# RWKV chain: the output sums move to a PSUM bank alone, the state sums move to the bank of the other sums

## The chip, the cores and the metric

The kernel runs as one program on one core of a Trainium2 chip. The metric is the device time of one execution in microseconds (us). Three runs of the kernel before took 1316.70, 1319.14 and 1324.66 us, so the median is 1319.14 us. The execution that the profile shows took 1316.68 us, of which 1314.9 us are the span from the first instruction of the program to the last.

## What is computed

One layer of a streaming encoder, for a prompt of 1024 positions and for 64 new positions with a past of 512. A projection gives the columns of three branches: an RWKV-7 recurrence (A), attention with forget gates (B) and sparse attention over selected keys (C, whose selection is a top-k search). The branches are gated, concatenated and multiplied by an output matrix. The change lies in the recurrence of branch A, which the reference states step by step:

```
def step(S, inp):
    r_t, w_t, k_t, v_t, kk_t, a_t = inp
    sa = einsum('bhij,bhj->bhi', S, -kk_t)
    S = S * w_t + sa (kk_t * a_t) + v_t k_t          # outer products
    return S, einsum('bhij,bhj->bhi', S, r_t)
wkv, y = lax.scan(step, wkv0, ...)
```

There are 8 heads of 64 by 64 state. The kernel takes 64 positions (a chunk) at a time, so that a step of its chain is four products for one pair of heads, and the next chunk needs the state that this one leaves.

## The kernel before, in words

The program lists instructions in an order of its own. A scheduler then puts the instructions of each engine in a fixed order of issue; it puts a ready instruction ahead of one whose inputs it expects later, and it sets semaphore waits between engines. It treats two accesses by different engines to one tile in PSUM as dependent when they lie in the same bank, even where they touch different columns, so a matmul into a bank waits until a read of that bank that stands ahead of it is done. On the chip each engine issues strictly in that order.

The time from about 160 to 760 us is a weave of several parts, started by `program` through `braid`. There are 17 units of four chunks (16 of the prompt, one of the new positions), and in each round of the loop run: `chain` of one unit, `chunk_invert` and `value_rows` of the next, `prepare` of the one after (`elem`, `chunk_rows`), and `tail` of the one before. Beside them `topk` searches the 256 best keys of branch C on DVE and ACT, and then writes one mask for each block of queries (lines L656 to L669, seven masks, of widths from 1024 down to 384, and 576 for the new positions). Between all of these, `pump` lays down pieces of the big projection (L154, three matmuls for each piece) on PE. `tied` keeps such a piece, and a piece of the search, from being issued ahead of the part that it was laid behind.

One step of `chain` does this, for a pair of heads, `h` being 0 and 1:

- **pa** (L1572): the old state times a chunk's rows, into bank gd; DVE adds a term to give `za` (L1573), while ACT scales the old state to `sp` (L1574).
- **pb** (L1577): `za` times the inverted matrix, into bank gd; DVE copies it in two halves to `UV` (L1582).
- **ps** (L1585): the sum that updates the state, into bank gc; DVE makes the new state `S` from it and `sp` (L1590).
- **py** (L1594) and **pyS** (L1596): two parts of the chunk's output, the second from the old state, into another part of bank gc. After four steps ACT copies all four outputs out at once to `Yt` (L1600).

The matmuls pa, pb and pyS have 64 by 64 weights, so each takes one quarter of PE's array; ps and py have 128 by 64, one half of it. All of them are float32, which the trace shows as two passes for each matmul, so a pair for both heads appears as x4.

Names that the rows and the order use: `ps_gc` and `ps_gd` are the tiles of the banks gc and gd; `BA`, `QR`, `UD`, `P` are operands of the chain; `ps_gb` with `U`, `T`, `Y`, `ND` (L1484, L1491, L1498, L1522, L1527, L1531) is `chunk_invert`; `ps_ga` (L107, L1376, L1425, L1434, L1470) is `prepare` and `value_rows`; `pproj` (L154) is the projection; `eq`, `cum`, `sg`, `nm` are the search's masks. PEld is the loading of weights into PE's array.

Of the kernel before, what the change touches and what calls it, by code (L numbers as in the profile page):

```python
# [18 lines left out]
OP = mybir.AluOpType  # L19
# [66 lines left out]
class K:  # L86
# [1461 lines left out]
    def chain(self, one, slots, x):  # L1548

        nc, I, O = self.nc, self.I, self.O  # L1550
        v, g, sc = nc.vector, nc.gpsimd, nc.scalar
        G = self.gring("gc", 1)
        hv = (slice(0, 64), slice(64, 128))
        i64 = self.con[:, C_I64:C_I64 + 64]
        QR, UD, P1, BA, UV, Pt = x["QR"], x["UD"], x["P1"], x["BA"], x["UV"], x["Pt"]
        sample = slots[0][1] == 16
        s0 = x.get("s0")
        if sample:
            send = one.tile([P, 256], F32, tag="e1", name="s_end").rearrange("p (c t) -> p c t", t=64)
        Yt = one.tile([P, 4, 64], F32, tag="Yt", name="Yt", bufs=2)  # L1560
        ends = []
        ch, ab = G(), self.gring("gd", 1)()
        for c, (hp, t) in enumerate(slots):
            S = s0[:, hp] if sample else self.state
            if t == 0:
                S = one.tile([P, 64], F32, tag="S", name="S", bufs=2)
                v.memset(S, 0.0)

            za, sp = [one.tile([P, 64], F32, tag=n, name=n) for n in ("za", "sp")]
            pa, pb = [ab[:, 256 * i + c * 64:256 * i + c * 64 + 64] for i in range(2)]  # L1570
            for h in range(2):
                nc.tensor.matmul(pa[hv[h]], QR[hv[h], c, 1], S[hv[h]], start=True, stop=True)  # L1572
            v.tensor_tensor(za, pa, P1[:, c], op=OP.add)  # L1573
            sc.activation(sp, S, AF.Copy, scale=Pt[:, c, 64:65])  # L1574
            yield
            for h in range(2):
                nc.tensor.matmul(pb[hv[h]], UD[hv[h], c], za[hv[h]], start=True, stop=True)  # L1577
            for h in range(2):
                if UA >> h & 1:
                    sc.copy(UV[hv[h], h, c], pb[hv[h]])  # L1580
                else:
                    v.tensor_copy(UV[hv[h], h, c], pb[hv[h]])  # L1582
            yield
            for h in range(2):
                nc.tensor.matmul(ch[hv[h], c * 64:c * 64 + 64], BA[:, h, c, 64 * h:64 * h + 64], UV[:, h, c], start=True, stop=True)  # L1585
            if sample:
                self.state = send[:, c]
            else:
                self.state = one.tile([P, 64], F32, tag="S", name="S", bufs=2)
            v.scalar_tensor_tensor(self.state, ch[:, c * 64:c * 64 + 64], Pt[:, c, 64:65], sp, op0=OP.mult, op1=OP.add)  # L1590

            py = ch[:, 256 + c * 64:320 + c * 64]
            for h in range(2):
                nc.tensor.matmul(py[hv[1 - h]], BA[:, h, c, 64 - 64 * h:128 - 64 * h], UV[:, h, c], start=True, stop=False)  # L1594
            for h in range(2):
                nc.tensor.matmul(py[hv[1 - h]], QR[hv[h], c, 0], S[hv[h]], start=False, stop=True)  # L1596
            if t >= 15:
                ends.append((hp, self.state))
            yield
        sc.copy(Yt, ch[:, 256:512].rearrange("p (c t) -> p c t", t=64))  # L1600
        if ends:
            ps = self.tp()
            n = len(ends)
            so = one.tile([64, n, P], F32, tag="QR" if sample else "so", name="so", bufs=3 if sample else 1)
            for i, (hp, s2) in enumerate(ends):
                nc.tensor.transpose(ps[0:64, i * P:i * P + P], s2, self.ident)
            sc.copy(so, ps[0:64, :n * P].rearrange("p (c t) -> p c t", t=P))
            dst = O["s_a_wkv" if sample else "p_a_wkv"][0, 0, 2 * slots[0][0]:2 * slots[0][0] + 2 * n]
            nc.sync.dma_start(out=dst.rearrange("(c h) v d -> v c h d", h=2), in_=so.rearrange("v c (h d) -> v c h d", h=2))
            yield  # L1610
        x.update(Yt=Yt)
# [318 lines left out]
```

## Time and profile before

| what | value |
|---|---|
| runs, median (lowest to highest) | 1319.14 us (1316.70 to 1324.66) |
| profiled execution | 1316.68 us |
| its span | 1314.9 us, so 1.8 us lie around it |
| PE (matmuls) busy | 1261.2 us, 96% of the span |
| DVE busy | 846.3 us, 64% |
| ACT busy | 781.1 us, 59% |
| POOL busy | 672.1 us, 51% |
| mean granted clock of PE | 0.984 |

The weave lasts from about 160 to 760 us. After it come the attention of branches B and C and the output products, up to the end. PE's busy time counts a matmul from its start to its modelled end, so overlapping matmuls count once. The granted clock is a share of full speed: 1.00 is 2.4 GHz, and half of it 1.2 GHz.

### The profile page before, as it was taken

What the parts mean: (1) busy time and instruction counts of PE and PEld (TensorE: products, weight loads), DVE (VectorE), ACT (ScalarE), POOL (GpSimd) and SP (SyncE); (2) the same over time, 40 slices, a digit from 0 to 9 for tenths busy, and PEclk for the clock granted to TensorE, in tenths of its full rate; (3) what the DMA queues carried; (4) which work ended last, traced back from release to release, by engine and by line L of the source; (5) the groups of instructions that cost most, each with busy time, mean ns of one, the idle gap of its engine ahead of it and who ended that gap; (6) DMA issues with size and microseconds to landing.
All of it is one profiled execution on the core that took longest, in us unless ns stands there. A gap on an engine that the chain in (4) does not pass through costs nothing.

```text
span 1314.9 us, 29369 instructions
## 1 busy us (share of the span) xinstructions
PE 1261.2 (96%) x10563; PEld 965.1 (73%) x10563; DVE 846.3 (64%) x2487; ACT 781.1 (59%) x1762; POOL 672.1 (51%) x973
## 2 busy tenths in 40 slices
PE   7999999999999999989999998999999988999997
PEld 5777777767777767767777677888888766777764
DVE  7378357887777678888654226555665588666642
ACT  7355357867777878534343356676665577655532
POOL 6333444544554556545463474567667477544311
PEclk9999999999999999988999998999999989999999
DMA  7432421232142325324243479777646475533323
GB/s 226 114 94 70 131 83 51 72 90 70 57 127 71 97 88 161 97 88 133 68 142 102 137 202 264 204 205 224 183 146 184 134 212 173 151 107 109 94 77 96
DMA packets 171700, 168.79 MB, mean 128 GB/s; under 512 B 38641, under 2 KB 146209, under 8 KB 171426
## 3 DMA queue, kind: packets, MB, share of 16 engines
q1 hardware_dynamic: 171554, 166.91, 43.7%
q8 instruction: 84, 1.38, 0.4%
q14 instruction: 62, 0.51, 0.1%
HBM read 106.18 MB, written 62.25 MB: 128 GB/s over the span
## 4 chain that ended last, share of the span: by engine, by line
PE 56%; DVE 7%; DMA 3%; ACT 3%; issue 1%; POOL 1%; SPq 0%; DVEq 0%; POOLq 0%; ACTq 0%
PE pproj L154 21%; PE pproj L1710 7%; PE ps_pv L995 5%; PE ps_atp L107 4%; PE ps_tp L1710 4%; PE ps_sc L964 2%; PE ps_sc L965 2%; PE ps_ga L1425 2%; PE ps_tp L107 1%; PE ps_gb L1484 1%; PE ps_gb L1491 1%; PE ps_gc L1594 1%; PE ps_gc L1585 1%; ACT junka L603 1%; PE ps_gc L1596 1%
## 5 line engine op out<-in xcount | busy, mean ns | idle before, releaser
L154 PE MATMUL pproj<-uH,wh 128*128 128x384 f32 (+4 forms) x1088 | 494.4, 454 | 0.0
L154 PE MATMUL pproj<-uH,wl 128*128 128x384 f32 (+4 forms) x1088 | 363.7, 334 | 0.0
L154 PE MATMUL pproj<-uL,wb 128*128 128x384 bf16 (+4 forms) x1088 | 358.9, 330 | 0.9 <-DVE shift L808 0.5
L154 PEld LDWEIGHTS pproj<-uH,wh 128*128 128x128 f32 (+1 forms) x1088 | 217.3, 200 | 4.1 <-issue 0.4
L154 PEld LDWEIGHTS pproj<-uH,wl 128*128 128x128 f32 (+1 forms) x1088 | 207.7, 191 | 2.4 <-issue 0.2
L154 PEld LDWEIGHTS <-wb 128*128 128x128 bf16 (+1 forms) x1088 | 106.3, 98 | 117.0 <-issue 80.4
L603 ACT ACTIVATE junka<-score,tk_tau 128x1024 f16<-128x1024 f32 (+4 forms) x160 | 149.3, 933 | 42.3 <-DVE tk_tau L617 26.4
L916 POOL TENSOR_SCALAR S<-S,mx 128x128 f32<-128x128 f32 (+8 forms) x136 | 105.0, 775 | 82.8 <-DVE mx L915 58.8
L140 POOL TENSOR_TENSOR wl<-wraw,wh 128x256 fp32r<-128x256 f32 (+1 forms) x184 | 137.6, 779 | 6.9 <-ACT wh L137 4.9
L933 ACT CAST hl<-ps_atp 128x512 fp32r<-128x512 f32 (+3 forms) x184 | 93.6, 515 | 80.0 <-PE ps_atp L107 71.0
L934 DVE TENSOR_TENSOR hl<-ps_atp,hl 128x512 fp32r<-128x512 f32 (+3 forms) x184 | 109.7, 600 | 45.6 <-ACT hl L933 43.9
L911 ACT ACTIVATE S<-S,mx 128x128 f32<-128x128 f32 (+8 forms) x136 | 105.8, 778 | 39.5 <-DVE mx L907 36.1
L995 PE MATMUL ps_pv<-hl,VS 128*128 128x256 f32 (+3 forms) x640 | 113.8, 290 | 7.2 <-ACT hl L933 3.1
L142 POOL TENSOR_SCALAR wb<-wraw 128x512 bf16<-128x512 f32 (+1 forms) x92 | 61.4, 685 | 106.7 <-issue 63.9
L995 PEld LDWEIGHTS ps_pv<-hl,VS 128*128 128x128 f32 (+1 forms) x640 | 90.6, 176 | 20.1 <-DVE hl L934 4.6
L107 PE MATMUL ps_atp<-ident,S 128*128 128x128 f32 x616 | 103.4, 279 | 1.1 <-POOL S L916 0.8
L1161 POOL TENSOR_TENSOR cb<-nm,T 128x256 f32<-128x256 bf16 (+2 forms) x80 | 56.3, 710 | 55.8 <-DVE mx L907 54.2
L107 PEld LDWEIGHTS ps_atp<-ident,S 128*128 128x128 f32 x616 | 76.3, 143 | 7.8 <-issue 1.7
L1710 PE MATMUL pproj<-oh,gh 128*128 128x512 f32 x144 | 67.4, 490 | 1.1 <-ACT oh L1689 0.8
L137 ACT CAST wh<-wraw 128x1024 fp32r<-128x1024 f32 (+1 forms) x46 | 47.7, 1037 | 33.0 <-PE pproj L154 32.4
L1710 PE MATMUL pproj<-ol,gb 128*128 128x512 bf16 (+1 forms) x144 | 52.4, 386 | 0.9 <-DVE ol L1690 0.9
L1710 PE MATMUL pproj<-oh,gl 128*128 128x512 f32 x120 | 46.7, 399 | 0.0
(383 smaller groups left out, 2834.1 us busy)
## 6 DMA issues: line engine op xcount, KB each, us to landing
wraw<-in_w_in_dram SPq DMA_DIRECT2D x45, 512.0 KB
oraw<-in_w_out_dram SPq DMA_DIRECT2D x12, 512.0 KB
out_dram<-rows SPq DMA_DIRECT2D x10, 512.0 KB
x<-in_x_prompt_dram SPq DMA_DIRECT2D x8, 512.0 KB
wt<-a_wa SPq DMA_DIRECT2D x16, 256.0 KB
b_v<-vs SPq DMA_DIRECT2D x8, 512.0 KB
VS<-b_v SPq DMA_DIRECT2D x8, 512.0 KB
d_y<-y SPq DMA_DIRECT2D x64, 64.0 KB
```

What stands on the lines that cost most here:

```text
L107: self.nc.tensor.transpose(out, x, self.ident[:n, :n])
L140: nc.gpsimd.tensor_tensor(l[:, k:k + 2, :n], raw[:, k:k + 2, :n], h[:, k:k + 2, :n], op=OP.subtract)
L142: nc.gpsimd.tensor_scalar(b[:, k:k + 4, :n], raw[:, k:k + 4, :n], 1.0, 0.0, op0=OP.mult, op1=OP.add)
L154: self.nc.tensor.matmul(ps[:n, :nt], a[:, k, :n], b[:, k, t0:t0 + nt], start=(k == 0 and i == 0), stop=(k == KD - 1 and i == 2))
L603: nc.scalar.activation(junk[:, :sc.shape[1]], sc, AF.Sign, bias=tf[:, j:j + 1], accum_out=cnt[:, j:j + 1])
L911: nc.scalar.activation(S[:, :kn], S[:, :kn], AF.Exp, bias=mx[:, nm - 1:nm], scale=-1.0, accum_out=mx[:, 6:7])
L916: nc.gpsimd.tensor_scalar(S[:, :kn], S[:, :kn], mx[:, 7:8], 0.5, op0=OP.mult, op1=OP.mult)
L933: nc.scalar.copy(ph[:kr, a:b], ps[:kr, a:b])
L934: nc.vector.tensor_tensor(pl[:kr, a:b], ps[:kr, a:b], ph[:kr, a:b], op=OP.subtract)
L995: nc.tensor.matmul(pv[0:m, q0:256], VS[:, kb, 0:m], hl[:, x, o:o + w], start=kb == 0 and x == 0, stop=at[-1][0] == last and n == 3)
L1161: nc.gpsimd.tensor_tensor(o, x, y, op=OP.add)
L1710: nc.tensor.matmul(ps[hf][:n, :], parts[m // 4][q][:, m % 4, :n], self.wo[m][q // 2][:, hf * 512:hf * 512 + 512], start=m == 0 and q == 0, ...
```

## The change

The chain had two PSUM tiles: `ch` in bank gc held the four state sums and the four outputs, and `ab` in bank gd the four pa and the four pb. Now `py4` in bank gc holds the four outputs alone. `ab` holds two pa and two pb, used in turn by even and odd steps, and the four state sums behind them. The arithmetic, the operands and the number of instructions on every engine are the same: each engine has the same instructions before and after, in another order.

```diff
-        ch, ab = G(), self.gring("gd", 1)()
+        py4, ab = G(), self.gring("gd", 1)()
...
-            pa, pb = [ab[:, 256 * i + c * 64:256 * i + c * 64 + 64] for i in range(2)]
+            pa, pb = [ab[:, 128 * i + c % 2 * 64:128 * i + c % 2 * 64 + 64] for i in range(2)]
+            ps = ab[:, 256 + c * 64:320 + c * 64]
...
-                nc.tensor.matmul(ch[hv[h], c * 64:c * 64 + 64], BA[:, h, c, 64 * h:64 * h + 64], UV[:, h, c], start=True, stop=True)
+                nc.tensor.matmul(ps[hv[h]], BA[:, h, c, 64 * h:64 * h + 64], UV[:, h, c], start=True, stop=True)
...
-            v.scalar_tensor_tensor(self.state, ch[:, c * 64:c * 64 + 64], Pt[:, c, 64:65], sp, op0=OP.mult, op1=OP.add)
-
-            py = ch[:, 256 + c * 64:320 + c * 64]
+            v.scalar_tensor_tensor(self.state, ps, Pt[:, c, 64:65], sp, op0=OP.mult, op1=OP.add)
+
+            py = py4[:, c * 64:c * 64 + 64]
...
-        sc.copy(Yt, ch[:, 256:512].rearrange("p (c t) -> p c t", t=64))
+        sc.copy(Yt, py4[:, :256].rearrange("p (c t) -> p c t", t=64))
```

Behind the changed place the lines are numbered two higher: pa is L1574 after, pb L1579, ps L1587, `S` L1592, py L1596, pyS L1598.

The first place is PE, the chain's 38th step, from ps to the next step's pa. Before:

```order
L1585 MATMUL ps_gc<-UV,BA 64x64 x2
L1491 LDWEIGHTS ND_1698
L1491 MATMUL ps_gb<-T_7810,ND_1698 128x64
...
L1425 MATMUL ps_ga<-QR,BK 128x128 x4
L1594 MATMUL ps_gc<-UV,BA 64x64 x2
L1596 MATMUL ps_gc<-S,QR 64x64 x2
L1572 MATMUL ps_gd<-S,QR 64x64 x2
```

With the change:

```order
L1596 MATMUL ps_gc<-UV,BA 64x64
L1587 MATMUL ps_gd<-UV,BA 64x64 x2
L1596 MATMUL ps_gc<-UV,BA 64x64
L1598 MATMUL ps_gc<-S,QR 64x64 x2
L1425 MATMUL ps_ga<-QR,BK 128x128 x4
L1491 LDWEIGHTS ND_1698
L1491 MATMUL ps_gb<-T_7810,ND_1698 128x64
...
L1574 MATMUL ps_gd<-S,QR 64x64 x2
```

The py and pyS matmuls moved up to the ps matmuls, and the same eight other matmuls that stood between ps and py now stand between pyS and the next pa.

The second place is DVE, where the search writes its first mask (width 1024). Before:

```order
L656 TENSOR_SCALAR eq,tk_need<-sg 128x1024
L1522 TENSOR_TENSOR Y_8843<-ps_gb,con 128x256
L1380 SCALAR_TENSOR_TENSOR QR<-zt,par,ps_ga 128x4x64
L1590 SCALAR_TENSOR_TENSOR S<-ps_gc,Pt,sp 128x64
L657 TENSOR_TENSOR tk_need<-tk_need,tk_cnt 128x1
L664 SCALAR_TENSOR_TENSOR cum<-one_383,eq 128x1024
L1384 TENSOR_TENSOR BK<-kp,Pi 128x4x64
L1391 SCALAR_TENSOR_TENSOR rk<-zt,par,kp 128x256
L1382 TENSOR_TENSOR BK<-QR,tha 128x4x64
```

With the change:

```order
L656 TENSOR_SCALAR eq,tk_need<-sg 128x1024
L1349 TENSOR_SCALAR ass<-ps_ga 128x4
L1522 TENSOR_TENSOR Y_8615<-ps_gb,con 128x256
L657 TENSOR_TENSOR tk_need<-tk_need,tk_cnt 128x1
L664 SCALAR_TENSOR_TENSOR cum<-one_383,eq 128x1024
L1359 SCALAR_TENSOR_TENSOR L<-con,lw 128x260
L658 TENSOR_SCALAR tk_need<-tk_need 128x1
L1584 COPY UV<-ps_gd 64x64 x2
L667 SCALAR_TENSOR_TENSOR sg<-cum,tk_need,sg 128x1024
L1531 TENSOR_TENSOR U_8649<-U_8581,ps_gb 128x256
L1592 SCALAR_TENSOR_TENSOR S<-ps_gd,Pt,sp 128x64
L669 TENSOR_SCALAR nm<-sg 128x1024
```

The mask stands earlier against the chain: the search's last mask (L669, 64x576) is behind the 50th new state of the chain before, and behind the 48th with the change; from the first L656 to that last mask DVE makes six new states before and five with the change.

## Rows read from the trace of the kernel before

**Rows 1.** The page: engines' busy time, and PE's granted clock in 40 slices.

```profile
PE 1261.2 (96%) x10563; PEld 965.1 (73%) x10563; DVE 846.3 (64%) x2487; ACT 781.1 (59%) x1762; POOL 672.1 (51%) x973
...
PEclk9999999999999999988999998999999989999999
```

**Rows 2.** Stretches: length, busy us of PE, PEld, DVE, ACT, POOL; granted clock, DMA.

```profile
160.00:560.00 400.00, 388.69 (x4459) 292.43 (x4459) 300.75 (x966) 297.43 (x679) 203.38 (x317) 1.00 0.29 88
560.00:620.00 60.00, 51.60 (x501) 38.54 (x497) 51.24 (x119) 23.40 (x57) 33.35 (x46) 0.83 0.38 114
```

**Rows 3.** PE's waits, 200 to 780 us: total us, times, longest us.

```profile
PE ps_ga L1434 <- DVE BA L1429: 4.8, 2, 2.5
...
PE ps_gc L1594 <- DVE S L1590: 0.9, 3, 0.4
...
PE ps_gc L1594 <- DVE s_end L1590: 0.6, 2, 0.5
```

**Rows 4.** Timeline of PEld: start us, us, operation, count; py, pyS and pa.

```profile
216.37 0.20 PEld L1594 LDWEIGHTS ps_gc<-UV,BA 128*64 128x64 f32 x4 [0.31 <-DVE S L1590]
216.63 0.14 PEld L1596 LDWEIGHTS ps_gc<-S,QR 64*64 64x64 f32 x2
216.65 0.14 PEld L1572 LDWEIGHTS ps_gd<-S,QR 64*64 64x64 f32 x2
...
216.91 0.10 PEld L154 LDWEIGHTS <-wb 128*128 128x128 bf16 x1
```

**Rows 5.** Timeline of PEld: one pyS and one pa that stand apart.

```profile
450.61 0.20 PEld L1596 LDWEIGHTS ps_gc<-S,QR 64*64 64x64 f32 x4
450.87 0.11 PEld L1606 LDWEIGHTS ps_tp<-ident,S 128*64 128x64 f32 x1
...
161.80 0.20 PEld L1572 LDWEIGHTS ps_gd<-S,QR 64*64 64x64 f32 x4 [0.17 <-issue]
162.07 0.19 PEld L154 LDWEIGHTS pproj<-uH,wl 128*128 128x128 f32 x1
```

**Rows 6.** Timeline of PEld: L1376 alone, then ps directly ahead of it.

```profile
299.38 0.41 PEld L1376 LDWEIGHTS ps_ga<-ident,arn 128*64 128x64 f32 x8 [0.18 <-issue]
299.96 0.19 PEld L154 LDWEIGHTS pproj<-uH,wl 128*128 128x128 f32 x1 [0.17 <-issue]
...
236.84 0.20 PEld L1585 LDWEIGHTS ps_gc<-UV,BA 128*64 128x64 f32 x4 [0.25 <-DVE shift L808]
236.96 0.42 PEld L1376 LDWEIGHTS ps_ga<-ident,arn 128*64 128x64 f32 x8
237.55 0.20 PEld L1484 LDWEIGHTS <-U 64*64 64x64 f16 x8 [0.17 <-issue]
```

**Rows 7.** Timeline of PEld: L1484 alone, then pb directly ahead of it.

```profile
190.87 0.20 PEld L1484 LDWEIGHTS <-U 64*64 64x64 f16 x8 [0.25 <-issue]
...
191.24 0.20 PEld L107 LDWEIGHTS ps_ga<-ident,BK 128*128 128x128 f32 x2
...
241.85 0.19 PEld L1577 LDWEIGHTS ps_gd<-za,UD 64*64 64x64 f32 x4 [0.20 <-issue]
...
242.36 0.10 PEld L154 LDWEIGHTS <-wb 128*128 128x128 bf16 x1
```

**Rows 8.** Timeline of all engines, inside the stretch of the masks.

```profile
567.82 0.41 DVE L1522 TENSOR_TENSOR Y<-ps_gb,con 128x256 f16<-128x256 f32 x1
...
568.28 0.31 PE L1484 MATMUL ps_gb<-Y,U 64*64 64x64 f16 x8 [1.58 <-DVE Y L1522]
```

**Rows 9.** Instructions by line: ns least/median/most, first and last start us.

```profile
L656 DVE TENSOR_SCALAR_CACHE_REDUCE eq<-sg x7: 543/819/1205, 556.9 to 614.4; 128x1024 f16<-128x1024 f16 x1, 128x896 f16<-128x896 f16 x1, 128x768 f16<-128x768 f16 x1, 128x640 f16<-128x640 f16 x1
...
L669 DVE TENSOR_SCALAR nm<-sg x7: 260/360/597, 568.6 to 624.7; 128x1024 bf16<-128x1024 f16 x1, 128x896 bf16<-128x896 f16 x1, 128x768 bf16<-128x768 f16 x1, 128x640 bf16<-128x640 f16 x1
...
L1585 PE MATMUL ps_gc<-UV,BA x272: 219/222/369, 207.7 to 744.5; 128*64 128x64 f32 x136
```

## The prediction

> **What bounds the kernel.** I read the busy shares first. PE is busy for 1261.2 of 1314.9 us [rows 1], so the time is PE's own work, plus 54 us in which it stands, plus what it loses at a lower clock. Then the stretches of the weave, since the change lies there. From 160 to 560 us PE is busy for 388.69 of 400 us at a granted clock of 1.00: 2.8% of idle time, while DVE is at 75% [rows 2]. From 560 to 620 us it is another picture: PE is busy for 51.60 of 60 us at a clock of 0.83, and DVE has gone up to 85%. So there are two regimes. In the first, only what occupies PE counts. In the second, PE waits for DVE: at 568.28 us a matmul of `chunk_invert` starts 1.58 us late because DVE's `Y` came only at 567.82 us [rows 8]. The seven masks of the search lie there, from 556.9 to 624.7 us [rows 9]. Then the waits: the one that the change removes, py for the read of the state sum in the same bank, costs PE 0.9 and 0.6 us in the whole weave [rows 3]. It is small, because the order of issue puts other matmuls between ps and py. Last, the timeline of weight loads, which shows what a group of small matmuls costs PE.
>
> **The change part by part.** Each engine has the same instructions as before, so no work goes away. What changes is their order, and with it which matmuls stand beside each other on PE. That has a price here: when the next matmul uses another cut of the array (128x128, 128x64, 64x64), its weights are loaded only after the group before has run through. I measure a group from its first load to the first load of the next.
>
> *The 128x64 groups.* Before, ps and py stood apart; py alone takes 216.37 to 216.63, 0.26 us [rows 4], and ps has the same shape. With the change py and ps stand together. What the second pair costs then is seen where ps stands ahead of L1376, which has the same cut: the two take 0.71 us (236.84 to 237.55), L1376 alone 0.58 us (299.38 to 299.96) [rows 6], so the pair adds 0.13 us in place of 0.26. Counted along PE's whole order, groups of this cut fall from 368 to 304. 64 x 0.13 = **8.3 us less**.
>
> *pyS and pa.* Before, pyS and the next pa stood side by side. They use four different quarters of the array, and the rows show them loaded within 0.02 us of each other: all of it takes 216.63 to 216.91, 0.28 us [rows 4]. Apart, pyS takes 0.26 us and pa 0.27 us [rows 5], so parting them costs 0.25 us. In the order they share a group in 59 of 68 steps before, and in 5 with the change: 54 x 0.25 = **13.5 us more**.
>
> *What comes back.* The groups of 64x64 rise only by 23 (251 to 274), not by 54, since 31 of the freed ones stand beside other matmuls of that cut. pb ahead of L1484 shows what it saves: together 0.51 us (241.85 to 242.36), L1484 alone 0.37 us (190.87 to 191.24) [rows 7], so pb adds 0.14 in place of 0.26 or 0.27 us. 31 x 0.12 = **3.7 us less**. The groups of 64x128 rise by 3 (48 to 51); a split group costs at most another small group's 0.26 us, so 0 to 0.8, of which I take **0.4 us more**. The number of 128x128 groups, 488, stays.
>
> The rows' sum is 13.5 - 8.3 - 3.7 + 0.4 = **+1.9 us**. The Trainium skill, "TensorEngine Tiling (Array Packing)", Key Properties, says that a change of tiling mode drains the engine and that different tiles work in parallel. By the first half alone one would count groups: 1165 before and 1127 with the change, which would make it a gain of some 38 x 0.13 = 4.9 us. The second half speaks against the change, and the trace bears it out with 0.28 against 0.53 us, so I keep +1.9.
>
> *The wait.* py's wait goes, 1.5 us in all [rows 3]. But the next pa needs `S` itself, and now stands as the first matmul that does. It has the same eight other matmuls ahead of it that py had in the place shown. So the wait moves: a gain of 1.5 us if pa is never late, and as much lost again if it is late twice as often. I take **-0.5**. The Trainium skill, "Perfetto Trace Analysis", Optimizing Tensor Performance, advises rotating independent groups through banks so that a read overlaps the next matmuls; by that rule alone the whole 1.5 us would be saved, 1.0 us below my sum. Behind PE's waiting pa stands the projection; it is not needed soon. Three other new neighbours in bank gd cost nothing: ps comes after the copies to `UV` that it needs anyway, pa after the `S` that it needs anyway, and a slot that comes round after two steps was read long ago. The copy to `Yt` (ACT) no longer has the state sums in its bank.
>
> *The masks.* The search now runs up to two or three steps ahead of the chain, and its masks meet other parts of the units: the first no longer stands among the products of `elem` (L1380 to L1391). The sum of DVE's work is the same, so I take **0**. The bounds are the two rivals below: -16.9 and +17.6 us.
>
> Behind the weave PE's order is the same but for some 110 of 3,600 instructions of attention and output that change places; I take 0 for them. SP's order shifts with them, and no DMA is added.
>
> Sum against the profiled execution: 1316.68 + 1.9 - 0.5 = **1318.1 us**. That execution was at the low end of the runs; the median is 1319.14, 2.5 us higher. I give **1318**.
>
> **The rivals.**
>
> *A, faster: the stretch of the masks clears.* From 560 to 620 us PE stood for 8.4 us, and a clock of 0.83 means that 34% of it, 20.4 us, ran at 1.2 GHz instead of 2.4, which loses 10.2 us of work: 18.6 us in all [rows 2]. At the rate of the stretch before it would lose 2.8% of 60, or 1.7 us. If the masks fall on lighter parts of the units, and `S` no longer holds py back, up to 16.9 us go: 1301.2. For it: the first mask's new neighbours on DVE are few. Against it: DVE's work is not less, and the second mask takes over those products.
>
> *B, slower: the masks press closer.* From the first L656 to the last L669 DVE now makes five new states instead of six, so about one step's work of PE is no longer there to stand beside the same masks. A step takes (744.5 - 207.7) / 67 = 8.0 us [rows 9]. Where DVE is the bound, PE stands for that much more in this stretch, and there each us of standing came with 10.2 / 8.4 = 1.2 us lost to the clock: 8.0 x 2.2 = 17.6 us, 1335.7. It decides once DVE's 85% in the stretch leaves no gap of its own, so that each mask delays `chunk_invert`. Against it: PE's projections are laid at the same pace, and DVE still had 9 us free in 60.
>
> *C: the groups do not save what I count.* If py and ps in the mixed order (py, ps, ps, py) still cost 0.26 us each, and the 31 neighbours save nothing because one of the two waits, 8.3 + 3.7 us are not given back: 1330.1, likelier half of it, about 1324.
>
> That the change does nothing is excluded: the order shows py ahead of `S`.
>
> **How the numbers follow.** Forecast 0.67, with its own range of 1309 to 1327 (half of what the masks can do either way). A 0.14, B 0.11, C 0.08. A change under 1% (13 us) is about what a measurement of this kernel cannot tell from none. A gives the chance of faster, 0.14. B and a little of C, 0.03, lie above 1%: slower 0.14. The forecast and the rest of C are within it: 0.72. The range of 1304 to 1331 holds the forecast and C, a third of A and a sixth of B, and leaves out 0.18.
>
> **What would show it.** Right: in the profile after, a group of py and ps takes about 0.39 us and a lone pyS about 0.26; py waits for nothing on DVE, and pa has a wait of 1 to 2 us in total in its place; from 160 to 560 us PE stays at 97% busy and the chain's last ps comes within 8 us of 744.5. Wrong: PE's idle time or its clock between 540 and 640 us differ by over 8 us from the 8.4 and 10.2 here (A or B), a group of py and ps of 0.5 us (C), or new stretches of a lower clock in the attention, where I counted nothing.

## The result, and the profile after

The changed kernel takes 1326.57 us in the median of 19 runs (1320.76 to 1331.05), the kernel before 1317.56 us in 19 runs beside it (1312.04 to 1325.86). The ratio is 1.0061, with a 95% interval of 1.0047 to 1.0076: the change costs about 8 us (6 to 10). That is within 1%, and inside the range, but it is a slowdown where I forecast none.

The profiled execution took 1322.52 us. Its page answers to [rows 1]:

```profile
PE 1259.3 (95%) x10563; PEld 963.6 (73%) x10563; DVE 843.8 (64%) x2487; ACT 779.8 (59%) x1762; POOL 666.0 (50%) x973
...
PEclk9999999999999999999999998999999989999999
```

The instructions are the same in number, and PE is busy for 1.9 us less than before, while the span grew by 5.8 us. So PE stands more. The windows say where; the third is new here. The columns are the length, then busy time with instructions of PE, PEld, DVE, ACT and POOL, the granted clock, the DMA share and GB/s. The kernel after:

```profile
160.00:560.00 400.00, 384.55 (x4347) 289.80 (x4345) 296.66 (x950) 292.95 (x667) 198.89 (x309) 0.99 0.29 87
560.00:620.00 60.00, 50.59 (x573) 37.94 (x571) 51.36 (x136) 27.19 (x68) 35.87 (x47) 0.94 0.32 97
620.00:760.00 140.00, 135.63 (x1480) 101.02 (x1480) 68.27 (x207) 52.81 (x131) 68.76 (x105) 1.00 0.37 117
```

The kernel before, whose first two stretches are [rows 2], in the third:

```profile
620.00:760.00 140.00, 138.22 (x1485) 103.18 (x1485) 69.13 (x212) 54.80 (x134) 69.49 (x104) 1.00 0.35 108
```

PE's idle time went from 11.3 to 15.5 us in the first stretch, from 8.4 to 9.4 in the second and from 1.8 to 4.4 in the third: 7.7 us more, and most of it outside the stretch of the masks. Not all of it belongs to the change. The run e1 below, whose order of issue is that of the kernel before, stands 11.8, 9.8 and 3.9 us there, so only the first stretch stands clearly longer with the change. The list of PE's waits from 160 to 760 us has 51 cases with 28.4 us in sum, against 33 with 20.3 us before. These lead it (what PE waited for: us in total, times, longest), where [rows 3] had py's wait:

```profile
PE ps_gb L1491 <- ACT T L1536: 3.6, 6, 1.5
PE ps_gd L1579 <- DVE za L1575: 3.1, 3, 2.6
PE ps_ga L107 <- DVE BK L1384: 2.7, 2, 1.9
PE ps_gb L1484 <- DVE Y L1522: 2.6, 6, 1.2
PE ps_gc L1596 <- DVE UV L1584: 2.1, 5, 1.2
```

None of these is a wait for a bank. Each is for the result of a VectorE or ScalarE instruction that came late. The longest of them shows how such a wait comes about. First VectorE in the changed kernel, then PE:

```profile
587.11 1.49 DVE L664 TENSOR_TENSOR_SCAN cum<-one,eq 128x640 f16<-128x640 f32 x1 [2.25 <-DMA d_nm<-nm]
588.51 0.20 DVE L1575 TENSOR_TENSOR za<-ps_gd,P 128x64 f32<-128x64 f32 x1
588.63 0.41 DVE L1436 SCALAR_TENSOR_TENSOR vb<-ps_ga,QR 128x256 f32<-128x256 f32 x1
```

```profile
585.83 0.34 PE L154 MATMUL pproj<-uH,wl 128*128 128x384 f32 x1
588.77 0.33 PE L1579 MATMUL ps_gd<-za,UD 64*64 64x64 f32 x4 [2.60 <-DVE za L1575]
```

The order put the search's scan (L664) ahead of `za`. The scan waited 2.25 us for a transfer of an earlier mask, and `za`, behind it in VectorE's queue, waited with it, and so did pb on PE. This is one case, and not the whole loss: it lies in the stretch of the masks, where PE stands for 9.4 us here and for 9.8 us in e1.

The prices of the groups came out as read. A group of ps and py, and the lone pyS behind it, on PEld in the kernel after:

```profile
216.78 0.20 PEld L1587 LDWEIGHTS ps_gd<-UV,BA 128*64 128x64 f32 x4
216.89 0.20 PEld L1596 LDWEIGHTS ps_gc<-UV,BA 128*64 128x64 f32 x4
217.16 0.20 PEld L1598 LDWEIGHTS ps_gc<-S,QR 64*64 64x64 f32 x4
217.42 0.10 PEld L154 LDWEIGHTS <-wb 128*128 128x128 bf16 x1
```

ps and py together take 0.38 us (216.78 to 217.16), pyS alone 0.26 us. From 170 to 560 us the medians are 0.382 us in 39 cases and 0.262 us in 31.

### The profile page after: what moved, and what is told of

The parts are those of the page before. It is cut to its first block, busy times and chain, and to the rows that moved or that the text cites. A ratio compares the mean times of both kernels' runs of the same rounds, so it can differ in the third digit from the quotient of the medians.

```text
span 1320.7 us, 29383 instructions
## 1 busy us (share of the span) xinstructions
PE 1259.3 (95%) x10563; PEld 963.6 (73%) x10563; DVE 843.8 (64%) x2487; ACT 779.8 (59%) x1762; POOL 666.0 (50%) x973
## 4 chain that ended last, share of the span: by engine, by line
PE 78%; DVE 8%; DMA 6%; ACT 3%; issue 3%; POOL 2%; SPq 0%; DVEq 0%; POOLq 0%; ACTq 0%
PE pproj L154 35%; PE pproj L1712 7%; PE ps_pv L995 5%; PE ps_atp L107 4%; PE ps_tp L1712 4%; PE ps_ga L1425 3%; PE ps_sc L964 2%; PE ps_sc L965 2%; PE ps_gb L1484 2%; PE ps_tp L107 1%; PE ps_gb L1491 1%; ACT junka L603 1%; PE ps_gc L1596 1%; PE ps_gd L1579 1%; PE ps_gc L1598 1%
## 5 line engine op out<-in xcount | busy, mean ns | idle before, releaser
L1161 POOL TENSOR_TENSOR cb<-nm,T 128x256 f32<-128x256 bf16 (+2 forms) x80 | 49.6, 625 | 53.4 <-DVE mx L907 45.5
L137 ACT CAST wh<-wraw 128x1024 fp32r<-128x1024 f32 (+1 forms) x46 | 47.7, 1037 | 28.5 <-PE pproj L154 28.2
L1430 POOL TENSOR_SCALAR ND<-BN 64x256 f16<-64x256 f32 x34 | 13.7, 403 | 74.4 <-DVE BN L1429 67.7
```

Source lines behind the costliest of these rows:

```text
L1161: nc.gpsimd.tensor_tensor(o, x, y, op=OP.add)
```

## The experiments

Two theories remained after the traces, and a third to exclude.

- **O**, the order: the scheduler, freed from py's wait, laid the work of VectorE and ScalarE differently, and PE now waits for late results.
- **G**, the groups: parting pyS from pa costs PE more than my +1.9 us.
- **B**, the banks themselves: the new places cost something on the chip.

All runs are timed in five rounds beside the kernel before. An order of issue is imposed by a dependency without a semaphore between neighbours on an engine; after and before have the same instructions, so the order of one can be laid on the other.

**e1 and two mixed orders.** The edit of e1, on the changed kernel, with the list of the old order of all five engines:

```diff
+    for names in json.loads(zlib.decompress(base64.b85decode(ORDER))):
+        names = [f"I-{n}" for n in names if f"I-{n}" in at]
+        for a, b in zip(names, names[1:]):
+            tc.add_manual_dep(at[b], a, mybir.DependencyInfo(mybir.DependencyClass.NoSync, mybir.DependencyReason.DATA), reason="order of issue")
```

`ORDER` holds one list for each engine, and `at` finds an instruction by its name.

> The changed kernel with its two banks, but all five engines held to the order of issue of the kernel before (a table of that order, given to the scheduler). Theory O (the changed order makes PE wait more often for DVE and ACT, and that is most of the +8 us) and theory G (parting pyS from pa costs PE more than I counted) both expect the time of the kernel before, less at most the 1.5 us of the wait: -1.5 to 0 us against before, ratio 0.999 to 1.000. Theory B (the two banks themselves cost time on the chip, whatever the order) expects the slowdown to stay: +6 to +9 us.

1319.33 against 1316.68 us, ratio 1.0015 (0.9991 to 1.0039). No cost of the new banks with the old order can be told from none, and the 6 to 9 us of B lie outside the interval. So B falls as the cause of the 8 us, though e1 alone would allow up to 5 us. The loss lies in the order of issue, of whichever engine, PE's groups included. The windows of e1, first and third:

```profile
160.00:560.00 400.00, 388.22 (x4463) 292.38 (x4463) 301.06 (x966) 297.24 (x679) 202.95 (x319) 1.00 0.29 88
...
620.00:760.00 140.00, 136.08 (x1451) 100.91 (x1450) 65.21 (x203) 55.06 (x136) 70.84 (x106) 1.00 0.35 109
```

The list of PE's waits from 160 to 760 us sums to 24.3 us in e1, and to 20.3 us in the kernel before, which has the same order of issue. The two executions differ in the granted clock of the masks' stretch (0.94 and 0.83); whether that makes the difference is not shown. So 24.3 us is the fairer number to set beside the 28.4 us of the changed kernel, whose clock was 0.94 there too.

e2 imposes the old order on VectorE and ScalarE alone (its `ORDER` holds these two lists), and leaves the rest to the scheduler.

> The changed kernel with DVE and ACT held to the order of the kernel before; PE, POOL and SP are ordered freely. PE's groups are then worse than in the changed kernel: 315 of 128x64 and 281 of 64x64, pyS and pa together in 2 steps; by the prices of my prediction +4.7 us against before (57 x 0.25 - 27 x 0.12 - 53 x 0.13, and 6 more groups of 128x128 at about 0.1). Theory O expects just that, +3 to +5.5 us against before, as the extra waits are gone. Theory G (the groups cost the +8 us) expects +9 to +13 us. Theory B expects +8 us or more.

1338.94 us, ratio 1.0165 (1.0139 to 1.0190). e3 is its mirror: the banks of before, with VectorE and ScalarE in the changed kernel's order.

> The kernel before, with its old banks, but DVE and ACT held to the order of the changed kernel, so that the search runs one to three chain steps ahead; PE, POOL and SP are free. PE's groups stay as before (369 of 128x64, 247 of 64x64, pyS and pa together in 59 steps). Theory O expects +5 to +8 us against before. Theories G and B expect no change, -2 to +2 us.

1337.68 us, ratio 1.0165 (1.0138 to 1.0192). Both are 21 to 22 us slower than the kernel before. Only B's "+8 us or more" for e2 allowed so much, and e1 has ruled that out; so neither run tells O from G. What they do show is that the order of two engines, with the rest left to the scheduler, is worse than either whole order: PE's waits from 160 to 770 us sum to 31.2 us in e2 and 38.3 us in e3, against 24.3 (e1) and 28.4 us up to 760 us with the whole orders.

**e4 and e8: pyS beside pa again.** The changed kernel, with pyS issued directly behind the next step's pa; the scheduler is free otherwise. `old_state` issues the pyS pair of the step before and ties it behind pa by a dependency like that of e1. The last pyS of each unit has no next step there and is not tied:

```diff
                 nc.tensor.matmul(pa[hv[h]], QR[hv[h], c, 1], S[hv[h]], start=True, stop=True)
+            if c:
+                old_state(*last)
...
-            for h in range(2):
-                nc.tensor.matmul(py[hv[1 - h]], QR[hv[h], c, 0], S[hv[h]], start=False, stop=True)
+            last = (c, py, S)
```

> The changed kernel, with pyS of a step issued directly behind the next step's pa, so that they share the array again (54 steps) while ps and py stay together (69 groups of the two). Groups: 314 of 128x64, 235 of 64x64. By the prices of my prediction PE's own work falls by 7 to 8 us against before and by about 9 against the changed kernel. Theory G expects the whole of it: -6 to -10 us against before. Theory O expects the saving less the waits of its own new order, in which the search still runs about one step ahead: -7 to 0 us against before. Theory B expects it no better than before, 0 to +3.

1308.31 us, ratio 0.9932 (0.9908 to 0.9956): faster than both kernels. e8 repeats it for a trace.

> The version with pyS issued behind the next step's pa, once more, for its trace (the one of e4 can't be read beside the others). The time as in e4: ratio 0.993. Theory G: TensorE's own work from the first pa to the last py is 8 to 12 us below the changed kernel's 553.5, its idle time there near the changed kernel's 28 us. Theory O: the work falls by 3 at most, and the idle time comes back to the 21 us of the kernel before or below.

1308.54 us, ratio 0.9948 (0.9924 to 0.9972). From the first pa to the last py, taking from the length the time in which PE is idle and what the clock loses (the length times one less the granted clock), 543.2 us of work are left, against 553.5 in the changed kernel: 10 us less, as G said. The idle time is 26.1 us, near the changed kernel's 28.2, as G said too. So the groups are worth what the rows say. But here the scheduler made a new order as well, so it doesn't yet say what the groups cost in the change.

**e5, e6, e7: the groups alone, with the order held.** e5 has the old order everywhere, and on PE py directly behind ps. From PE's order, e1 against e5:

```
 L1587 MATMUL ps_gd<-UV,BA 64x64 x2
+L1596 MATMUL ps_gc<-UV,BA 64x64 x2
 L1484 LDWEIGHTS U_2462
...
-L1596 MATMUL ps_gc<-UV,BA 64x64 x2
 L1598 MATMUL ps_gc<-S,QR 64x64 x2
 L1574 MATMUL ps_gd<-S,QR 64x64 x2
```

> The changed banks with the old order on every engine, and one move on TensorE alone: each py pair stands directly behind its ps pair (they stood some 1.5 us apart). pyS stays beside the next step's pa, as before. 1083 groups of like-shaped small matmuls instead of 1165. Theory G (the number of groups on TensorE): 65 groups of 128x64 go, at 0.13 us each, and some 17 of 64x64 at 0.12, against the kernel before -8 to -11 us, ratio 0.992 to 0.994. Theory O (it is the order of VectorE and ScalarE that makes TensorE wait in the changed kernel): that order is the old one here, so no more waiting than before; O says nothing against G's gain, but if the py pairs' new place makes TensorE late for the steps that VectorE and ScalarE run in the old order, the gain goes again in waits: ratio 1.000 or above.

1313.44 against 1315.41 us, ratio 0.9978 (0.9956 to 1.0000). This lies between the two theories: G expected 0.992 to 0.994, O 1.000 or more. In e6, L1598 goes up behind L1596 as well.

> As the run before it, and pyS too moves up, directly behind py: TensorE then has the groups of the changed kernel (1123 against its 1127), while every other engine has the order of the kernel before. Against the kernel before, theory G alone (all of the +8 us is groups): ratio 1.006. The groups by the rows: -8.5 for py beside ps, +13 for 52 pyS taken from pa at 0.25, -2.5 for 64x64 groups merged with neighbours: +2 us, ratio 1.0015, and then theory O owes the other 6 us to the new order's waits. Against the first run of this call it shows the price of parting pyS from pa: 1123 - 1083 = 40 groups, at 0.25 us +10, at 0.13 us +5.

1320.44 us, ratio 1.0025 (1.0003 to 1.0047). With the changed kernel's groups on PE, and the old order elsewhere, about 3 us are lost by the ratio (0.4 to 6.2), not 8. e7 goes the other way: the changed kernel's own order, with 29 of the 68 pyS pairs moved down on PE behind the next pa.

> The changed kernel with its own order on every engine, except that 29 of the 68 pyS pairs move down on TensorE to stand directly behind the next step's pa (1104 groups against 1127). Theory G: 29 x 0.25 = -7 us less what a pyS lost beside another 64x64 neighbour (the count of groups falls by 23, at 0.13 us -3 at least): -3 to -7 against the changed kernel, ratio to the kernel before 1.001 to 1.004. Theory O alone: the order of VectorE and ScalarE is the changed kernel's, its waits stay, ratio 1.006.

1321.18 us, ratio 1.0035 (1.0019 to 1.0050), between the two, as G said: each engine but PE in the new order, and still 3 to 5 us won back for 23 groups (against 1.0061 and, in e9 below, 1.0072). The intervals meet, so the times alone leave this open. The trace speaks for it: reckoned as for e8, PE's work is 548.0 us, 5.5 below the changed kernel's, and its idle time 30.6 us.

**e9, e10, e11: the three side by side.** e5 and e6 lay close to the edge of what can be told apart, so the changed kernel, e6 and e5 ran once more on one chip.

> The changed kernel itself, unaltered, beside the next two on one chip, so that the three can be set against each other directly. Ratio to the kernel before 1.006, as in its first timing.

> e6 once more (TensorE's groups of the changed kernel, the old order on the other engines). If the order of the other engines owes more than half of the +8 us (theory O, as e6 alone says: 4.7 of 8): ratio 1.001 to 1.004, some 3 to 6 us below the changed kernel of this call. If the groups owe nearly all of it (theory G): the same as the changed kernel, ratio 1.005 to 1.007.

> e5 once more (old order, py directly behind ps, pyS still beside pa). As e5: ratio 0.996 to 1.000. By the count of groups alone (82 fewer at 0.13 us): 0.992. Between this run and the one before it lies the parting of pyS from pa alone, 40 groups: 5 us at 0.13, 10 us at 0.25.

| | median us | ratio to before (95%) | PE's waits, 160 to 760 us | last ps at us |
|---|---|---|---|---|
| before | 1316.18 | | 20.3 | 744.5 |
| e9, changed kernel | 1323.93 | 1.0072 (1.0044 to 1.0099) | 28.5 | 750.4 |
| e10, its groups in the old order | 1317.51 | 1.0003 (0.9985 to 1.0022) | 23.3 | 743.0 |
| e11, pyS left beside pa | 1309.07 | 0.9937 (0.9916 to 0.9959) | 27.7 | 735.2 |

In the row of before, the last two numbers are from its first profile. e9 and e10 have practically the same groups on PE (1127 and 1123) and differ in the order of all else, that of PE's other matmuls included. Their intervals do not meet: the order costs 6.4 us by the medians and 9 us by the ratios, and the list of PE's waits grows by 5.2 us. The first timing of the changed kernel and e6, which ran apart, give 4.7 us by the ratios. e10 and before differ in the groups and the banks: +0.4 us here (-2.0 to +2.9) and +3.3 in e6 (0.4 to 6.2), both by the ratios; by the medians 1.3 and 5.0. So O carries the larger part of the 8 us by the ratios, and G the rest, which may be nothing. From e11 to e10 lies the parting of pyS from pa: 8.4 us by the medians, and 7.0 from e5 to e6.

One caution: e5 and e11 are the same kernel, and their ratios are 0.4% apart (0.9978 and 0.9937). A difference of less than 5 us is safe only between runs of one set.

The windows of e10 against those of the kernel after above, in the first and third stretch:

```profile
160.00:560.00 400.00, 387.70 (x4469) 293.35 (x4468) 300.72 (x967) 296.66 (x678) 202.55 (x318) 1.00 0.29 88
...
620.00:760.00 140.00, 136.38 (x1462) 101.86 (x1454) 63.87 (x202) 55.11 (x136) 69.73 (x105) 0.99 0.35 107
```

PE is idle for 12.3 and 3.6 us here, and for 15.5 and 4.4 in the kernel after. So most of the standing that the order adds lies from 160 to 560 us, ahead of nearly all of the masks: PE's waits there sum to 10.9 us in e1, 11.6 in e6 and 11.5 in e10, and to 14.8 and 15.0 in the two executions of the changed kernel. The row that leads there is the one for ACT's copy `T`; e10 first, then the kernel after, from 160 to 560 us:

```profile
PE ps_gb L1491 <- ACT T L1536: 2.0, 4, 0.9
```

```profile
PE ps_gb L1491 <- ACT T L1536: 3.4, 5, 1.5
```

The place of the scan counts for less. PE stands for 9.0 us in the stretch of the masks in e10, against 9.4. In e10 the scan waits for its transfer for 0.6 us, and `za` makes PE's matmuls wait 0.2 us in all; the first line is from the waits of VectorE, the second from what waited for `za`:

```profile
DVE cum L664 <- DMA d_nm<-nm: 0.6, 1, 0.6
```

```profile
  PE ps_gd L1579: 0.2, 1
```

**e12: the late instructions moved up.** If single late instructions cost the time, moving them should give it back. VectorE's order, the changed kernel against e12, at the place shown above (two more places on VectorE and twelve on ScalarE are like it):

```
 L1531 TENSOR_TENSOR U_9096<-U_9017,ps_gb 128x256
+L1575 TENSOR_TENSOR za<-ps_gd,P_8228 128x64
 L664 SCALAR_TENSOR_TENSOR cum<-one_383,eq 128x640
-L1575 TENSOR_TENSOR za<-ps_gd,P_8228 128x64
 L1436 SCALAR_TENSOR_TENSOR vb<-ps_ga,QR 128x256
```

> The changed kernel with its own order, except for a few instructions that TensorE was seen to wait for, each moved up past work that nothing waits for. VectorE: two za move ahead of the search's scan (L664) in front of them, and U and the BK group ahead of the clearing of nm (L675), which stands waiting for a transfer. ScalarE: T's copy (L1536) moves ahead of Yt, sp, Pt and the search's count (L603) wherever Yt stands shortly before it. TensorE's order is the changed kernel's to the last row. Theory O in its plain form (single late instructions make TensorE wait, and each wait is lost time): the waits addressed are za 3.3 us, BK 2.1 (of which 1.3 can go), T 3.6, so -5 to -8 us against the changed kernel, ratio to the kernel before 1.000 to 1.003, and these rows go from the list of TensorE's waits. Theory G: ratio 1.006 to 1.007. A third way: the rows go, but TensorE, earlier by as much, waits at the next step instead (its waits in 160 to 760 stay near 28 us in sum): ratio 1.004 to 1.007.

1325.14 us, ratio 1.0063 (1.0039 to 1.0088): nothing is won. It went the third way. The waits moved away from are nearly gone, those for `T` among them, and others stand in their place:

```profile
PE ps_ga L1306 <- DVE vb L1436: 2.7, 1, 2.7
PE ps_ga L1306 <- ACT UV L1463: 2.3, 3, 1.6
...
PE ps_ga L107 <- DVE BK L1384: 0.7, 1, 0.7
...
PE ps_gd L1579 <- DVE za L1575: 0.5, 2, 0.3
...
PE ps_gb L1491 <- ACT T L1536: 0.3, 1, 0.3
```

The sum of the list is 28.4 us, the same as without the moves; from 160 to 560 us it is 16.3 us, against 14.8. At the place shown, e12's VectorE and PE read:

```profile
587.07 1.49 DVE L664 TENSOR_TENSOR_SCAN cum<-one,eq 128x640 f16<-128x640 f32 x1 [2.28 <-DMA d_nm<-nm]
588.48 0.40 DVE L1436 SCALAR_TENSOR_TENSOR vb<-ps_ga,QR 128x256 f32<-128x256 f32 x1
```

```profile
585.89 0.33 PE L1579 MATMUL ps_gd<-za,UD 64*64 64x64 f32 x4
588.93 0.58 PE L1306 MATMUL ps_ga<-wt,wabh 128*128 128x256 f32 x1 [2.71 <-DVE vb L1436]
```

pb now starts on time, at 585.89. But the scan waits for its transfer until 587.07 as before, and the next result behind it, `vb`, makes PE wait 2.71 us. At this place the loss is VectorE's queue standing at the scan, and not `za`'s place behind it.

## Why the prediction was wrong

The step that failed is **the wait**, taken as -0.5 us, together with the zero for the new order of everything else, which the prediction gives under the masks: "The sum of DVE's work is the same, so I take **0**". I asked only where py's own 1.5 us would go, and priced the new order at nothing because each engine's work stays the same. Measured, the order costs 6.4 us by the medians (e9 against e10). PE's waits sum to 28.4 and 28.5 us in the changed kernel, and to 23.3 to 24.3 us in e10, e6 and e1, where the other engines keep the old order. So 4 to 5 us of the cost are PE standing for late results, nearly all of VectorE and ScalarE; which engine's new order makes them late, no run shows. pa, where I looked for the wait, is late only once in the list of the changed kernel:

```profile
PE ps_gd L1574 <- DVE S L1592: 0.3, 1, 0.3
```

In the old order the wait did move to pa, as forecast. In e1 py no longer waits for the state, and pa does:

```profile
PE ps_gd L1574 <- DVE s_end L1592: 1.3, 3, 0.5
PE ps_gd L1574 <- DVE S L1592: 0.8, 1, 0.8
```

The 1318 has a slip besides, outside its terms. The sum says +1.4 us; I added it to the profiled execution, 2.5 us below the median, and so named a time below the median of the kernel before. From the median it would have been 1320.5 us.

The other steps:

- **What bounds the kernel** held, with one correction. I took 160 to 560 us as a stretch in which only what occupies PE counts. But most of the waits that the new order adds lie in just this stretch. And e5 and e11 took 82 groups from PE, and its waits rose from 24.3 us (e1, with the same order elsewhere) to 27.6 and 27.7 us: VectorE and ScalarE are close enough behind that PE soon waits for them.
- **The 128x64 groups** held in price: 0.382 us for the pair against two of 0.265 before, so 0.148 saved where I took 0.13.
- **pyS and pa** held in price: 0.262 us each when apart, 0.275 together (33 cases before). With the 64x64 neighbours and the split groups the forecast for parting them was 13.5 - 3.7 + 0.4 = 10.2 us; the runs gave 7.0 and 8.4.
- **The groups' sum**, +1.9 us, agrees with e10 and e6: +0.4 and +3.3 by the ratios, with 1.9 in both intervals. By the half of the Trainium skill's rule that counts changes of the tiling mode ("TensorEngine Tiling (Array Packing)", Key Properties) it would have been a gain of 4.9 us; neither run shows one. The half on tiles working in parallel decides here, as the trace of before had said.
- **The rotation of banks.** The 1.5 us that the Trainium skill's advice on rotating banks ("Perfetto Trace Analysis", Optimizing Tensor Performance) would have saved did not come: in e1, with the new banks and the old order, the ratio is 1.0015 and its interval begins at 0.9991, which is -1.2 us.
- **The masks** were neither rival. Their premise came true: from the first L656 to the last L669 it is now 53.9 us (553.4 to 607.3), and 67.8 before (63.4 in e1, in the same order). But the stretch from 560 to 620 us lost 9.4 us to standing and 3.6 to the clock (0.94), so 13.0 in place of 18.6. B's price did not come. Nor is the better clock the change's: e1, in the old order, also has 0.94 there.

```profile
560.00:620.00 60.00, 50.23 (x549) 37.78 (x547) 55.09 (x128) 24.83 (x61) 36.13 (x48) 0.94 0.40 121
```

- **C** is excluded: py and ps take 0.382 us together, and its other half, the neighbours, falls too. In the kernel after, pa and L1484 in one group take 0.51 us (6 cases from 170 to 560 us), and 0.26 and 0.37 us alone.
- **What would show it.** My signs missed the failure. "The last ps within 8 us of 744.5" was kept, at 751.2, though those 6.7 us are all that this execution lost. "97% busy from 160 to 560" was the one that spoke: 96.1%, or 4.1 us more of standing. I asked for the waits of py and pa, and should have asked for the sum of all of PE's waits, in more than one execution.

Two things stay open. In the traces of e9 and e10 the stretch from the first pa to the last py differs by 7.8 us, of which 4.1 is PE's idle time; the clock went the other way by 1.7 us. So about 5 us lie where the trace calls PE busy. The ends of matmuls are modelled there, so short stands between queued matmuls may hide in them, but no run shows that. And no run parts the search's pace from the other moves in the new order: e12 shows that VectorE's stand at the scan, and not `za`'s place, costs those 2.6 us, but not what the scan's place costs over the whole weave. PE stands for 9.0 to 9.8 us in the stretch of the masks in e1, e10 and both executions of the changed kernel, which speaks against that place as the main source.

## What to carry to other kernels

When an edit frees a scheduler, price the order that it makes on all engines, also where the work of each stays the same; the sum of all waits of the engine that bounds the kernel, before and after, is the number to ask for, and one more execution of the old order (e1) tells how much of its growth is the order's. To tell the edit from the order, lay the old order on the new kernel (e1), and then move one group at a time (e5, e6): an order imposed on two engines, with the rest left to the scheduler (e2, e3), cost more than either whole one and told little. And a result that came late in a queue was not mended by moving it up where what stood ahead of it waited for a transfer: the next in the queue took over the wait (e12).

## What was not expected

Moving late instructions forward (e12) left the sum of PE's waits at 28.4 us to the tenth, in 54 cases instead of 51. The same order of issue gave a granted clock of 0.83 in one execution (the kernel before) and 0.94 in another (e1, the new banks in that order) in the stretch of the masks. And small matmuls of one cut on four quarters of the array are worth keeping together: four of them cost 0.275 us, two and two apart 0.524, and with pyS tied behind pa (e4, e8) the changed kernel runs in 1308.5 us, 7 to 9 us below the kernel before.
